# Group weight sums of a down-projection: GpSimd subtractions against DMAs that add from DRAM

## The chip, the cores and the metric

One Trainium2 chip, and of it one core. The metric is the device time of one execution of the whole kernel in microseconds (us). A profile of one execution is taken beside the timed runs. The engines are TensorE (PE; its weight loads PEld), VectorE (DVE), ScalarE (ACT), GpSimd (POOL) and SyncE (SP), each with an instruction queue of its own that is worked in order; SP, ACT and POOL also issue DMAs.

## The reference

One layer of a decoder trunk on 1024 tokens of width 1024, in float32: a norm, two attentions whose outputs are gated and merged, a residual add, then a norm and a gated MLP with a short causal convolution, a residual add, and a last norm. The change lies in the last product of the MLP:

```python
def conv_ffn(xn, w_up, conv_w, conv_b, w_down):
    S = xn.shape[1]
    u = xn @ w_up
    upad = jnp.pad(u, ((0, 0), (CONV_WIDTH - 1, 0), (0, 0)))
    c = conv_b
    for j in range(CONV_WIDTH):
        c = c + upad[:, j:j + S] * conv_w[j]
    gate, val = jnp.split(c, 2, axis=-1)
    return (jax.nn.silu(gate) * val) @ w_down      # 1024x2816 times 2816x1024
...
        x = x + conv_ffn(xn, w_up[l], conv_w[l], conv_b[l], w_down[l])
    return rmsnorm(x, norm_final_w)
```

## The kernel before, in words

All data lie transposed: channels on the 128 partitions, tokens along the free dimension. Each float32 product is made of three matmuls on rounded parts: high weight by high operand, high weight by low operand, low weight by high operand. A weight tile of 128x1024 (`raw`) gets its high part `wh` by a cast on ScalarE (L161) and its low part `wl` by a subtraction on VectorE (L163); `wh` and `wl` have two buffers each, so a weight can be split once the group two before it is done on TensorE. Operands are split into `h` in the same way, by halves of 128x512 (L835 on ScalarE, L836 on VectorE).

The down-projection (`down`) has 22 chunks of hidden channels. Six are multiplied plainly (`pieces`, L1117). The other sixteen form a 2x2 block product by a Strassen-like scheme with seven products, the stages P1, P5, P6, P3, P7, P2, P4 in this order. Each stage has four groups m (128 output channels each), and each group 8 x 3 matmuls of 128x512 (`product`, L1166). The weight of a stage is a quarter of the weight matrix or a sum of quarters, the operand a quarter of the hidden values or a sum of quarters. With A11, A12 the upper quarters (left, right) and A21, A22 the lower ones as the code's `quarter(m, right, below)` addresses them, where `right` picks the later hidden chunks and `below` the later output channels:

- P5 takes S1 = quarter(left, below) + quarter(right, below). `group_first` makes it in tile `S` (one of four buffers, one for each m): a load from SP (L112), then a DMA from GpSimd's queue that adds from DRAM (L113).
- P6 takes S2 = S1 - quarter(left, above), P3 takes S4 = quarter(right, above) - S2, P7 takes S3 = quarter(left, above) - quarter(left, below). `group_raw` loads the quarters into `raw` buffers (three of them) through SP (L151), and `group_sum` subtracts on GpSimd (L99 for P6, L101 for P3, L104 for P7), in place in `S` for P6 and P3 and in place in a `raw` buffer for P7.
- P1, P2 and P4 take plain quarters, loaded into `raw`.

`next_w` hands out the next weight and `ahead` prepares two groups in advance, with the raw loads of one more. `prep` makes the operands, two a group: `operand` sums hidden quarters in place on VectorE (L1031 for P5, L1033 for P6, L1038 for P7, L1042 for P4) and `parts_h` splits the result into one of 20 `h` buffers. The hidden quarters come from DRAM through SP (`fetch_h`, L1009) into `ha`, `hb`, `hc`, eight buffers each. After a group its sum is added to the output tile `x3` (`evict`, L1173), and where an output is complete, `norm` squares it on ScalarE (L1155), adds the squares on VectorE (L1157) and scales by the norm weight on ScalarE (L1158). The running sum of squares, `acc`, takes an `S` buffer once the first of them is free; the squares take tiles `c` of 128x1024, of which there are two (before, the convolution used them).

The order of the instructions on each engine is fixed when the kernel is built, by a planner: it simulates the kernel with costs of its own and takes, of what is ready on an engine, that which stands first in the program. So operands of a later stage can run in an earlier one (the P4 operands of L1042 ran in P5), and loads are issued as soon as their buffers are free. The waits on the chip follow from the real times; an instruction whose input is late holds all that is queued behind it on its engine.

Of the kernel before, what the change touches and what calls it, by code (L numbers as in the profile page):

```python
# [13 lines left out]
ALU = mybir.AluOpType  # L14
# [3 lines left out]
P = 128  # L18
# [4 lines left out]
H2 = 512  # L23
# [20 lines left out]
class Trunk:  # L44
# [24 lines left out]
    def ahead(self, n):  # L69
        while len(self.wq) < n and self.wsrc and (self.wsrc[0][1] != "pair" or self.uw):  # L70
            src, nk, *eng = self.wsrc.pop(0)
            if nk == "grp":
                self.wq.append(self.load_w(None, 8, raw=self.group_sum(*src, eng[0] if eng else self.group_raw(*src))))
            elif nk == "pair":
                first, skip = eng or (False, 0)
                self.wq.append(self.split_pair(*self.sum_pair(src, first), skip))
            else:
                self.wq.append(self.load_w(src, nk, *eng))
        if self.deep and self.wsrc and len(self.wsrc[0]) == 2 and not isinstance(self.wsrc[0][1], str):

            src, nk = self.wsrc[0]
            self.wsrc[0] = src, nk, None, None, self.load_raw(src, nk)
        elif self.deep and self.wsrc and self.wsrc[0][1] == "grp" and len(self.wsrc[0]) == 2:
            src, nk = self.wsrc[0]
            self.wsrc[0] = src, nk, self.group_raw(*src)

    def quarter(self, m, right, below):
        return self.w_dn[m + 4 * below, :, N1 + 8 * right:N1 + 8 * right + 8, :]

    def group_raw(self, name, m):  # L90

        parts = {"P5": (), "P6": ((0, 0),), "P3": ((1, 0),), "P7": ((0, 0), (0, 1))}[name]
        return [self.load_raw(self.quarter(m, *p), 8) for p in parts]

    def group_sum(self, name, m, raws):

        s, tt = self.S[m], self.nc.gpsimd.tensor_tensor
        if name == "P6":
            tt(s, s, raws[0], ALU.subtract)  # L99
        elif name == "P3":  # L100
            tt(s, raws[0], s, ALU.subtract)  # L101
        elif name == "P7":
            s = raws[0]
            tt(s, s, raws[1], ALU.subtract)  # L104
        return s

    def group_first(self, m):

        nc = self.nc
        s = self.tl(self.uw, [P, KC, P], "S", bufs=4)  # L110
        flat = lambda t: t.rearrange("p k c -> p (k c)")
        nc.sync.dma_start(flat(s), flat(self.quarter(m, False, True)))  # L112
        nc.gpsimd.dma_start(flat(s), flat(self.quarter(m, True, True)), accum_op=ALU.add)  # L113
        self.S.append(s)

    def sum_pair(self, src, first=False, idle=None):


        nc = self.nc
        g = self.tl(self.wp, [P, 2, 4, P], "raw", bufs=RAW)  # L120
        nc.sync.dma_start(g.rearrange("p a k c -> p (a k) c"), src[0])
        v = self.tl(self.wp, [P, 2, 4, P], "raw", bufs=RAW) if first and not idle else self.tl(self.uw, [P, 2, 4, P], idle or "rv", bufs=2)
        nc.sync.dma_start(v.rearrange("p a k c -> p (a k) c"), src[1])
        sa, sb = (self.tl(self.sfp[0], [P, 2, 4, P], self.sfp[1]) for _ in range(2))
        tt = nc.gpsimd.tensor_tensor
        tt(sa[:, 0], v[:, 0], v[:, 1], ALU.add)  # L126
        tt(sa[:, 1], sa[:, 0], g[:, 0], ALU.subtract)  # L127
        tt(sb[:, 0], g[:, 0], v[:, 0], ALU.subtract)  # L128
        tt(sb[:, 1], g[:, 1], sa[:, 1], ALU.subtract)
        return g, v, sa, sb  # L130
# [895 lines left out]
    def operand(self, stage, k):  # L1026

        tt, R = self.nc.vector.tensor_tensor, self.R
        a = R["B11", k]
        if stage == "P5":  # L1030
            tt(a, R["B12", k], a, ALU.subtract)  # L1031
        elif stage == "P6":
            tt(a, R["B22", k], a, ALU.subtract)  # L1033
        elif stage == "P3":
            a = R["B22", k]
        elif stage == "P7":
            a = R["B12", k]
            tt(a, R["B22", k], a, ALU.subtract)  # L1038
        elif stage == "P2":
            a = R["B21", k]  # L1040
        elif stage == "P4":
            tt(a, R["B21", k], a, ALU.subtract)  # L1042
        self.B[stage, k] = self.parts_h(a)

    def glu(self, j, w, us, tp, after):
# [29 lines left out]
    def down(self):  # L1075

        nc, tc = self.nc, self.tc
        with ExitStack() as ctx:
# [6 lines left out]
            tt = nc.vector.tensor_tensor  # L1085
# [60 lines left out]
            acc = []  # L1146

            def norm(m, hf, a=0, b=H2):

                if not acc:  # L1150
                    acc.append(self.tl(self.uw, [P, 2, H2], "S", bufs=4))
                x = x3[:, m, hf * H2 + a:hf * H2 + b]
                sum_ = acc[0][:, hf, a:b]
                sq = sum_ if m == 0 else self.tl(self.cpl, [P, b - a], "c")
                nc.scalar.activation(sq, x, AF.Square)  # L1155
                if m and (m < KC - 1 or hf):
                    tt(sum_, sum_, sq, ALU.add)  # L1157
                nc.scalar.mul(x, x, self.vecs[:, C_NO + m:C_NO + m + 1])  # L1158
                return sq
# [10 lines left out]
            def evict(ps, to, done):  # L1170
                for m, hf in to:
                    x = col(m, hf)
                    tt(x, x, ps, ALU.add)  # L1173
                    if done:
                        norm(m, hf)
# [36 lines left out]
            for a, b in ((0, q), (q, H2)):  # L1212
                for m, w in zip((2, 3), ws):
                    ps = chains[1][m][:, a:b]
                    product(ps, w, "P4", False, a, b, lambda k, m=m: tail.pop(0)() if a and k == (4 if m < 3 else 2) else None)
                    for f in owed:
                        f()
                    owed = []
                    x = x3[:, m + 4, a:b]
                    tt(x, x, ps, ALU.add)  # L1220
                    sq = norm(m + 4, 0, a, b)
                    while not a and tail:
                        tail.pop(0)()
                tail = self.last_norm(psD, [acc[0][:, 0, a:b], sq], x3, 0, a, b, ((0, 1, nc.vector), (1, 3, nc.vector), (6, 8, nc.gpsimd), (3, 6, nc.vector)) if a else
                                      ((0, 3, nc.gpsimd), (3, 5, nc.vector), (5, 8, nc.vector)))
# [98 lines left out]
```

## Time and profile before

| | us |
|---|---|
| median of 3 runs | 1338.62 |
| lowest and highest | 1336.24, 1339.04 |
| the profiled execution | 1338.15 |
| its span in the profile | 1336.4 |
| first matmul of P1, of P5, of P6, of P3, of P7 (us from the span's start) | 1164.0, 1185.7, 1208.5, 1230.2, 1257.0 |

How to read the rows that follow: in the waits, "engine line waited for" is followed by total us, times and the longest in us. In a table of stretches each engine has its busy us and number of instructions; then come the granted clock of TensorE as a share of full speed, the mean busy share of the 16 DMA engines, and GB/s. In a timeline a row has start, duration, engine, line, operation, tiles (out<-in) and number; in brackets the idle time before it and what ended it. In a group row, the busy us and the mean ns of one stand behind the bar, then the idle time before. DMA issues are listed with their number, size and the median us from issue to landing.

### The profile page before, as it was taken

The numbers are of one execution on the slowest core, as the hardware profiler recorded it, in microseconds if no ns is written. First come the engines' busy times: TensorE is split into PE (matmuls) and PEld (weight loads), VectorE is DVE, ScalarE is ACT, GpSimd is POOL, SyncE is SP. The second block draws the span as 40 slices with busy tenths as digits, with TensorE's granted clock in tenths as the row PEclk, the third lists the DMA queues.
The fourth block names the chain that finished last, engine by engine and source line by source line (L and its number), as shares of the span: only waits on it lengthen the run. The fifth ranks groups of instructions, "written<-read, shape, count | busy, mean of one in ns | idle before, by whom it ended". The sixth has DMA issues, their size and how long they took to land.

```text
span 1336.4 us, 17027 instructions
## 1 busy us (share of the span) xinstructions
PE 1317.7 (99%) x6256; PEld 1097.9 (82%) x6256; DVE 1064.3 (80%) x1429; ACT 606.2 (45%) x937; POOL 503.1 (38%) x364
## 2 busy tenths in 40 slices
PE   8999999999999999999999999999999999999997
PEld 6888888888888878888888888888888888888786
DVE  7847776289888976445669999999999997889664
ACT  8432232276667774333444343434343434334443
POOL 0346652000101015641446666666656620135111
PEclk9999999999999999999999999999999999999998
DMA  7244443976554246324423122222222229934242
GB/s 259 107 146 159 148 151 126 266 179 186 146 137 141 83 137 225 120 106 142 146 92 110 64 94 80 80 78 89 86 79 79 75 96 354 270 116 129 64 148 104
DMA packets 63091, 180.26 MB, mean 135 GB/s; under 512 B 6944, under 2 KB 16800, under 8 KB 63008
## 3 DMA queue, kind: packets, MB, share of 16 engines
q1 hardware_dynamic: 50976, 159.90, 36.4%
q10 hardware_dynamic: 11456, 17.18, 3.5%
q0 software_dynamic: 576, 2.10, 0.8%
q8 instruction: 49, 0.80, 0.2%
q14 instruction: 34, 0.28, 0.1%
HBM read 130.39 MB, written 48.76 MB: 134 GB/s over the span
## 4 chain that ended last, share of the span: by engine, by line
PE 95%; DVE 2%; ACT 1%; issue 1%; DMA 0%; POOLq 0%; POOL 0%; ACTq 0%
PE t L916 44%; PE y L1166 6%; PE g L182 4%; PE g L183 4%; PE g L184 4%; PE d L1166 4%; PE sc L184 3%; PE sc L183 3%; PE sc L182 3%; PE sc L648 3%; PE y L1117 2%; PE d L1117 2%; PE t L664 1%; DVE h L836 1%; PE t L767 1%; PE t L309 1%
## 5 line engine op out<-in xcount | busy, mean ns | idle before, releaser
L1060 POOL TENSOR_TENSOR us<-us,rstd 128x1024 f32<-128x1024 f32 x42 | 92.3, 2216 | 82.4 <-DVE us L481 47.6
L1069 ACT ACTIVATE c<-us,vecs 128x1024 f32<-128x1024 f32 x44 | 54.8, 1247 | 127.2 <-POOL us L1060 121.6
L161 ACT CAST wh<-raw 128x1024 fp32r<-128x1024 f32 (+1 forms) x53 | 53.9, 1016 | 102.3 <-PE sc L183 35.5
L142 DVE TENSOR_TENSOR sl<-sf,sh 128x1024 fp32r<-128x1024 f32 x62 | 89.3, 1441 | 12.8 <-ACT sh L140 12.8
L163 DVE TENSOR_TENSOR wl<-raw,wh 128x1024 fp32r<-128x1024 f32 (+1 forms) x53 | 70.4, 1331 | 36.3 <-ACT wh L161 26.6
L140 ACT CAST sh<-sf 128x1024 fp32r<-128x1024 f32 x62 | 64.5, 1042 | 61.6 <-PE t L916 44.0
L126 POOL TENSOR_TENSOR sf<-rv 128x512 f32<-128x512 f32 x30 | 50.4, 1681 | 93.5 <-DVE sl L142 59.0
L1166 PE MATMUL y<-h,wh 128*128 128x512 f32 (+1 forms) x288 | 80.8, 366 | 0.0
L1071 DVE SCALAR_TENSOR_TENSOR c<-us,vecs,c 128x1024 f32<-128x1024 f32 x44 | 74.4, 1724 | 5.8 <-ACT c L1069 5.7
L128 POOL TENSOR_TENSOR sf<-raw,rv 128x512 f32<-128x512 f32 x30 | 56.8, 1892 | 46.3 <-DVE sl L142 46.3
L1072 DVE SCALAR_TENSOR_TENSOR c<-us,vecs,c 128x1024 f32<-128x1024 f32 x44 | 73.2, 1697 | 0.0
L182 PE MATMUL g<-xh,wh 128*128 128x512 f32 x176 | 71.0, 403 | 1.5 <-ACT g L577 1.5
L183 PE MATMUL g<-xl,wh 128*128 128x512 f32 x176 | 70.3, 400 | 0.0
L184 PE MATMUL g<-xh,wl 128*128 128x512 f32 x176 | 70.2, 399 | 0.0
L1052 ACT ACTIVATE c<-c 128x1024 f32<-128x1024 f32 x22 | 23.4, 1063 | 88.5 <-DVE c L1072 88.5
L631 POOL MEMSET aT<- 128x128 f32 x32 | 6.1, 204 | 151.6 <-PE t L677 63.1
L652 DVE CUSTOM_DVE_ANT_0 L<-sc,bias 128x128 f32<-128x128 f32 (+7 forms) x64 | 47.8, 752 | 16.6 <-PE sc L648 13.7
L1166 PE MATMUL d<-h,wh 128*128 128x512 f32 x192 | 60.6, 397 | 0.0
L142 DVE TENSOR_TENSOR wl<-raw,wh 128x1024 fp32r<-128x1024 f32 (+1 forms) x32 | 59.7, 1864 | 0.1
L1166 PEld LDWEIGHTS y<-h,wh 128*128 128x128 f32 x288 | 52.1, 189 | 8.8
L127 POOL TENSOR_TENSOR sf<-sf,raw 128x512 f32<-128x512 f32 x31 | 58.2, 1876 | 2.2
L653 ACT ACTIVATE L<-L,sm 128x128 f32<-128x128 f32 (+7 forms) x64 | 49.6, 778 | 20.0 <-DVE sm L652 17.3
(413 smaller groups left out, 4282.0 us busy)
## 6 DMA issues: line engine op xcount, KB each, us to landing
u<-qd SPq DMA_DIRECT2D x72, 256.0 KB, 6.6
raw<-in_w_down SPq DMA_DIRECT2D x28, 512.0 KB, 3.5
raw<-in_w_up SPq DMA_DIRECT2D x23, 512.0 KB, 3.5
raw<-in_w_in SPq DMA_DIRECT2D x22, 512.0 KB, 4.1
hd<-c SPq DMA_DIRECT2D x22, 512.0 KB, 2.6
rv<-in_w_up SPq DMA_DIRECT2D x21, 512.0 KB, 3.5
gr<-gd SPq DMA_DIRECT2D x16, 512.0 KB, 3.4
qd<-us SPq DMA_DIRECT2D x15, 512.0 KB, 2.6
```

The lines of the kernel that those rows point to most:

```text
L127: tt(sa[:, 1], sa[:, 0], g[:, 0], ALU.subtract)
L140: cast = nc.scalar.copy(hi, src)
L142: low = nc.vector.tensor_tensor(lo, src, hi.bitcast(F32), ALU.subtract)
L163: self.lo = (eng or nc.vector).tensor_tensor(wl, raw, wh.bitcast(F32), ALU.subtract)
L182: nc.tensor.matmul(ps, wh[:, kc + o, :], ah, start=first and n == 0, stop=False)
L183: nc.tensor.matmul(ps, wh[:, kc + o, :], al, start=False, stop=False)
L184: nc.tensor.matmul(ps, wl[:, kc + o, :], ah, start=False, stop=last and n == len(kcs) - 1)
L916: nc.tensor.matmul(ps, (ah, ah, al)[p][:, k, :], (bh, bl, bh)[p], start=first and n == p == 0, stop=last and p == 2 and n == len(ks) - 1, ...
L1060: i = (nc.vector if m % NF == 0 else nc.gpsimd).tensor_tensor(us[:, 2:], us[:, 2:], self.rstd, ALU.mult)
L1071: nc.vector.scalar_tensor_tensor(c, us[:, 1:T + 1], cw[1], c, ALU.mult, ALU.add)
L1072: nc.vector.scalar_tensor_tensor(c, us[:, 0:T], cw[0], c, ALU.mult, ALU.add)
L1166: nc.tensor.matmul(ps, v[:, k, :], x, start=start and k == i == 0, stop=k == 7 and i == 2, skip_group_check=True)
```

## The change

The sums are made in place in `S` by DMAs that add from DRAM, issued on GpSimd's queue right after the split of the group's weight is traced. After P5, `S` (S1) changes sign on ScalarE and quarter(left, above) is added: it holds -S2. After P6, quarter(right, above) is added: S4. After P3, SP loads quarter(left, below) into `S`, ScalarE changes its sign and quarter(left, above) is added: S3. As P6 now takes -S2, its operand changes sign too, and P4's operand, which is made from it, adds where it subtracted. No sum is made on GpSimd itself any more, and the groups use no `raw` buffers and no loads ahead. Since `S` is now in use until P7, the running sum of squares and the squares move to two tiles `c`: `acc[0]`, and `acc[1]` whose two halves take turns.

```diff
             if nk == "grp":
-                self.wq.append(self.load_w(None, 8, raw=self.group_sum(*src, eng[0] if eng else self.group_raw(*src))))
+                name, m = src
+                self.wq.append(self.load_w(None, 8, raw=self.S[m]))
+                self.group_next(name, m)
...
-        elif self.deep and self.wsrc and self.wsrc[0][1] == "grp" and len(self.wsrc[0]) == 2:
-            src, nk = self.wsrc[0]
-            self.wsrc[0] = src, nk, self.group_raw(*src)
...
-    def group_raw(self, name, m):
-
-        parts = {"P5": (), "P6": ((0, 0),), "P3": ((1, 0),), "P7": ((0, 0), (0, 1))}[name]
-        return [self.load_raw(self.quarter(m, *p), 8) for p in parts]
-
-    def group_sum(self, name, m, raws):
-
-        s, tt = self.S[m], self.nc.gpsimd.tensor_tensor
-        if name == "P6":
-            tt(s, s, raws[0], ALU.subtract)
-        elif name == "P3":
-            tt(s, raws[0], s, ALU.subtract)
-        elif name == "P7":
-            s = raws[0]
-            tt(s, s, raws[1], ALU.subtract)
-        return s
+    def add_to(self, s, src):
+        flat = lambda t: t.rearrange("p k c -> p (k c)")
+        self.nc.gpsimd.dma_start(flat(s), flat(src), accum_op=ALU.add)
...
     def group_first(self, m):
 
-        nc = self.nc
         s = self.tl(self.uw, [P, KC, P], "S", bufs=4)
-        flat = lambda t: t.rearrange("p k c -> p (k c)")
-        nc.sync.dma_start(flat(s), flat(self.quarter(m, False, True)))
-        nc.gpsimd.dma_start(flat(s), flat(self.quarter(m, True, True)), accum_op=ALU.add)
+        self.nc.sync.dma_start(s, self.quarter(m, False, True))
+        self.add_to(s, self.quarter(m, True, True))
         self.S.append(s)
 
+    def group_next(self, name, m):
+
+        nc, s = self.nc, self.S[m]
+        if name == "P7":
+            return
+        if name == "P3":
+            nc.sync.dma_start(s, self.quarter(m, False, True))
+        if name != "P6":
+            nc.scalar.mul(s, s, -1.0)
+        self.add_to(s, self.quarter(m, name == "P6", False))
...
         elif stage == "P6":
-            tt(a, R["B22", k], a, ALU.subtract)
+            tt(a, a, R["B22", k], ALU.subtract)
...
         elif stage == "P4":
-            tt(a, R["B21", k], a, ALU.subtract)
+            tt(a, R["B21", k], a, ALU.add)
...
                 if not acc:
-                    acc.append(self.tl(self.uw, [P, 2, H2], "S", bufs=4))
+                    acc.extend(self.tl(self.cpl, [P, 2, H2], "c") for _ in range(2))
                 x = x3[:, m, hf * H2 + a:hf * H2 + b]
                 sum_ = acc[0][:, hf, a:b]
-                sq = sum_ if m == 0 else self.tl(self.cpl, [P, b - a], "c")
+                sq = sum_ if m == 0 else acc[1][:, m % 2, a:b]
```

## The prediction

> **What bounds the kernel now.** First the page's head, then what TensorE waited for, over the whole span.
>
> ```profile
> span 1336.4 us, 17027 instructions
> PE 1317.7 (99%) x6256; PEld 1097.9 (82%) x6256; DVE 1064.3 (80%) x1429; ACT 606.2 (45%) x937; POOL 503.1 (38%) x364
> ...
> PE t L309 <- ACT wh L339: 4.7, 1, 4.7
> PE d L1166 <- DVE wl L163: 3.5, 2, 3.0
> ```
>
> TensorE is busy all but 18.7 us. GpSimd work is worth nothing by itself; the change can pay only where GpSimd makes TensorE wait. The second wait is such a place: the grouped down-projection (L1166) waits twice for VectorE's low part of a weight (wl). Next, busy time by stretches, cut where the matmuls turn from one stage to the next: P5, P6, P3, P7.
>
> ```profile
> core 0: us, PE busy (x) PEld busy (x) DVE busy (x) ACT busy (x) POOL busy (x), PEclk, DMA share, GB/s
> 1185.70:1208.40 22.70, 22.18 (x98) 18.02 (x97) 20.48 (x21) 8.94 (x14) 11.57 (x4) 1.00 0.49 151
> 1208.40:1230.20 21.80, 21.80 (x97) 17.76 (x96) 19.77 (x20) 8.64 (x13) 11.88 (x4) 1.00 0.38 115
> 1230.20:1257.10 26.90, 23.89 (x99) 19.33 (x98) 19.18 (x23) 12.04 (x19) 3.85 (x2) 0.94 0.23 73
> 1257.10:1278.90 21.80, 21.80 (x98) 18.06 (x97) 15.92 (x20) 12.03 (x19) 4.80 (x2) 1.00 0.46 145
> ```
>
> The stages hold 96 matmuls each. P6 and P7 take 21.8 us without a gap; P5 takes 0.9 more, P3 5.1 more. That 6.0 us is all there is to win here. P3's 5.1 is 3.0 idle (26.90 - 23.89) and 2.1 of slower matmuls (23.89 - 21.80), as TensorE's timeline and clock show:
>
> ```profile
> 1235.78 0.61 PE L1166 MATMUL d<-h,wh 128*128 128x512 f32 x2
> 1239.41 0.50 PE L1166 MATMUL d<-h,wl 128*128 128x512 f32 x1 [3.01 <-DVE wl L163]
> ...
> 1240.87 1.06 PE L1166 MATMUL d<-h,wh 128*128 128x512 f32 x2
> ...
> 1243.39 0.62 PE L1166 MATMUL d<-h,wh 128*128 128x512 f32 x2
> ...
> 1240.00:1244.00 4.00, 4.00 (x12) 0.58 0.13 51
> ```
>
> Why was wl late? VectorE's timeline up to it, with two undisturbed rows, then GpSimd's:
>
> ```profile
> 1181.33 1.23 DVE L163 TENSOR_TENSOR wl<-S,wh 128x1024 fp32r<-128x1024 f32 x1 [0.17 <-ACT wh L161]
> ...
> 1226.00 3.40 DVE L163 TENSOR_TENSOR wl<-S,wh 128x1024 fp32r<-128x1024 f32 x1 [0.21 <-ACT wh L161]
> 1229.33 4.70 DVE L836 TENSOR_TENSOR h<-hb,h 128x512 fp32r<-128x512 f32 x4
> ...
> 1235.76 2.46 DVE L836 TENSOR_TENSOR h<-hc,h 128x512 fp32r<-128x512 f32 x1
> 1238.14 1.21 DVE L163 TENSOR_TENSOR wl<-S,wh 128x1024 fp32r<-128x1024 f32 x1
> ...
> 1254.35 2.49 DVE L836 TENSOR_TENSOR h<-hc,h 128x512 fp32r<-128x512 f32 x4
> ```
>
> ```profile
> 1190.80 3.98 POOL L99 TENSOR_TENSOR S<-S,raw 128x1024 f32<-128x1024 f32 x1 [5.38 <-DVE wl L163]
> ...
> 1225.91 2.42 POOL L104 TENSOR_TENSOR raw<-raw,raw 128x1024 f32<-128x1024 f32 x1 [3.71 <-DMA raw<-in_w_down]
> 1228.27 3.40 POOL L101 TENSOR_TENSOR S<-raw,S 128x1024 f32<-128x1024 f32 x1
> ...
> 1235.30 2.38 POOL L104 TENSOR_TENSOR raw<-raw,raw 128x1024 f32<-128x1024 f32 x1 [3.62 <-DMA raw<-in_w_down]
> ```
>
> Whenever a GpSimd sum runs, one VectorE instruction beside it loses about 2 us: 3.40 for 1.23 (2.2), 4.70 for four at 2.49 (2.2), 2.46 for 0.62, a quarter of that (1.8). Together 6.2 us. Without them the late wl would start at 1238.14 - 6.2 = 1231.9 and end at 1233.2; TensorE wanted it at 1239.41 - 3.01 = 1236.4.
>
> **The change, part by part.** *GpSimd sums out.* Twelve go:
>
> ```profile
> L101 POOL TENSOR_TENSOR S<-raw,S 128x1024 f32<-128x1024 f32 x4 | 13.8, 3446 | 8.1 <-DVE wl L163 8.1
> L99 POOL TENSOR_TENSOR S<-S,raw 128x1024 f32<-128x1024 f32 x4 | 11.6, 2890 | 30.1 <-DVE wl L163 30.1
> L104 POOL TENSOR_TENSOR raw<-raw,raw 128x1024 f32<-128x1024 f32 x4 | 9.6, 2399 | 33.4 <-DMA raw<-in_w_down 33.4
> ```
>
> The 35.0 us of GpSimd was never waited for directly, so its own worth is 0; its worth is the VectorE time. P3's stall goes whole (margin 1236.4 - 1233.2 = 3.2 us), and with it the slow matmuls: 5.1 us. P5's stall hangs on this piece of the chain that ended last:
>
> ```profile
> 1188.98 0.61 DVE h L836
> 1189.61 3.04 DMA hc<-hd
> 1192.67 1.58 DVE ha L1042
> ```
>
> That split frees the buffer which the load fills. VectorE was about 2 us late there by the same kind of collision, and the sum at 1190.80 disturbs the operand behind it again. With two times 2 us back against a gap of 0.52, the 0.9 us go too. Next on VectorE is nothing: its 20.5, 19.8 and 19.2 us in the three stages, less some 2 us for each of ten sums, leave about a third of it idle.
>
> *ScalarE sign turns in.* Eight (four after P5, four after P3), priced by these rows of the page:
>
> ```profile
> L1069 ACT ACTIVATE c<-us,vecs 128x1024 f32<-128x1024 f32 x44 | 54.8, 1247 | 127.2 <-POOL us L1060 121.6
> L161 ACT CAST wh<-raw 128x1024 fp32r<-128x1024 f32 (+1 forms) x53 | 53.9, 1016 | 102.3 <-PE sc L183 35.5
> ```
>
> So 1.0 to 1.25 us each; I take 1.25, the row with a scale in it. Four make 5.0 us in a stage where ScalarE is busy 9 to 12 us of 21.8. Behind a sign turn stand the next cast (wh) and the h casts. A weight buffer comes free one group (21.8 / 4 = 5.44 us) before its use, the wl is used only two matmuls (2 x 21.8 / 96 = 0.45 us) into its group, and cast (1.0) and wl (1.23) take, with their handovers, about 2.4 us; that leaves 5.44 + 0.45 - 2.4 = 3.5 us, which covers one sign turn. Cost 0; without that cover up to 8 x 1.25 = 10 us. After P5 the turn waits for VectorE's wl, which is due earlier than now.
>
> *Loads.* SP loses 16 loads of raw and gains four of S after P3, each waiting for that group's wl. On SP behind them stand loads of the P2 and P4 weights, which have three free raw buffers and tens of us: cost 0. GpSimd's queue gains 12 adding DMAs.
>
> ```profile
> raw<-in_w_down SPq DMA_DIRECT2D x28, 512.0 KB, 3.5
> ...
> S<-in_w_down SPq DMA_DIRECT2D x4, 512.0 KB, 6.0
> S<-in_w_down POOLq DMA_DIRECT2D x4, 512.0 KB, 9.7
> ...
> L113 POOL DMA_DIRECT2D S<-in_w_down x4: 862/882/1061, 1152.7 to 1161.1; - x4
> ...
> DMA to landing us min/median/max: 8.2/9.7/11.9
> ```
>
> Issuing takes 0.9 us, 10.6 in all, with nothing behind on that queue but further adds and the norm's rstd, stages later. No adding DMA runs in a quiet stretch, so its landing is bounded by a plain load (3.5) and the slowest add (11.9, in the busiest stretch); I take 9.7, its own row. Chain to the next stage: after P5, 1.25 + 0.9 + 9.7 = 11.9 us; after P6 less; after P3, with a reload of 3.5 to 6.0, 15.4 to 17.9. From a group's wl to the cast of the same group one stage on there are 21.8 - 2.4 = 19.4 us, 22.9 before TensorE waits. Covered: cost 0.
>
> *Signs, norm tiles.* The P6 and P4 operands stay one VectorE instruction each. The norm's squares alternate between two halves of one tile where two buffers alternated, 5.4 us apart in use: cost 0, or 0.6 us (an add of 128x512, half a wl) where one had to wait.
>
> **Sum.** 1338.15 (profiled execution; span 1336.4) - 5.1 - 0.9 = 1332.15. That execution lies 0.5 below the median of 1338.62, so 1332.6 against the median. The one reading in doubt is the 2.1 us. The Trainium skill, "TensorE: Matmul & The Clock Gate", section "HAM oscillation — how this bites in real kernels", warns of idle gaps above about 3.4 us. Here 3.01 us of idleness stand before a granted clock of 0.58, so trace and figure differ; by the figure the slow stretch would have another cause and the sum would be 1334.7.
>
> **The rivals.** *A: the clock dip is not the stall's.* Then only 3.9 us go: 1334.7. Against it: the first matmuls after the gap are the slow ones. The page named above is what speaks for it.
>
> *B: ScalarE held by the reload.* The planner decides when the kernel is built whether the sign turn of a P3 group stands ahead of the next group's wh cast. If ahead, ScalarE sits through the reload and the groups form a loop: landing, turn 1.25, cast 1.05, wl 1.23, some 0.2 of handover. At 3.5 us landing it takes 7.2 against 5.44: 4 x 1.76 - 3.5 slack = 3.5 us given back, 1336.1, just inside no change. For it: the reload comes due (2.4 + 3.5 = 5.9 us after the buffer is free) close to the next cast (5.44). Against it: a planner that knows the 3.5 puts the cast first.
>
> *C: the same loop at the 6.0 us of S loads.* 9.7 against 5.44: 17 - 3.5 = 13.5 us, 1346.1, slower. It decides from a landing of 4.8 us, where the loss passes 6.0 + 2.7. Against it: 6.0 is from the busiest stretch; P3's DMA share is 0.23.
>
> *D: the adding chain after P3 is late.* At the slowest rows 7.1 + 1.25 + 1.06 + 11.9 = 21.3 of 22.9 us (7.1 is the slowest landing of the S loads); twice the middle landings, 2 x (6.0 + 9.7) + 2.1 = 33.5, would start P7 10.6 us late, with another clock dip of 2.1 at 1332.6 + 12.7 = 1345. The 7.1 is here:
>
> ```profile
> L112 SPq DMA_DIRECT2D S<-in_w_down x4: 382/383/430, 1147.4 to 1148.9; - x4
> ...
> DMA to landing us min/median/max: 4.6/6.0/7.1
> ```
>
> Four issues took at most 1.06 us beside a busy VectorE. The Trainium skill, "SBUF — State Buffer", section "A bandwidth-pool intuition that's wrong (but worth ruling out)", has a GpSimd-issued DMA go from 620 to 3100 ns beside some VectorE copies; by that, as an estimate, the 21.3 would be 23.8 and D would hold. The issue rows speak against it here.
>
> *E: nothing moves.* VectorE's order is planned anew and another late instruction takes the place of the sums: about 1338.
>
> **How the numbers follow.** A measurement of this kernel tells about 0.2% (2.7 us) from no change. Forecast 0.52, A 0.06: faster 0.58. B 0.15, E 0.07: same 0.22. C 0.14, D 0.06: slower 0.20. Forecast alone: 1330 to 1335 (all of the 6.0 and the runs' own 2.8 us spread below, A's price above). The range runs 1329.8 to 1341; what is left out is most of C and D and a little below.
>
> **What would show it.** In the changed profile: no L1166 wait of TensorE on wl; P5, P6 and P3 at 21.8 us with clock 1.00; wl from S near 1.23 us throughout and four h splits at 2.49; eight new ScalarE instructions of about 1.25; 16 adding DMAs. Wrong would be: ScalarE idle on the S load ahead of a wh cast (B, C), a wh cast waiting for an adding DMA (D), VectorE still slow with GpSimd idle, or a wl late behind a new order (E).

## The result, and the profile after

The changed kernel takes 1332.00 us in the median (1331.47 to 1332.21, 6 runs) against 1338.47 (6 runs of the kernel before beside it): a ratio of 0.9955, 95% interval 0.9943 to 0.9968. The profiled execution took 1331.87 us, its span 1330.1.

What TensorE waited for over the whole span of the changed kernel, longest first (total us, times, longest):

```profile
PE t L304 <- ACT wh L334: 5.1, 1, 5.1
PE g L177 <- ACT g L572: 1.5, 4, 0.5
PE d L200 <- POOL rs L194: 1.1, 1, 1.1
```

The wait of the grouped products on wl is gone from the list; the first entry is a wait at the start of the kernel that stood there before with 4.7 us. The stretches of P5, P6, P3 and P7 in the changed kernel (busy us and number of PE, PEld, DVE, ACT, POOL, then clock, DMA share, GB/s):

```profile
1185.70:1207.50 21.80, 21.80 (x98) 18.06 (x97) 15.07 (x22) 12.31 (x17) 3.46 (x4) 1.00 0.77 157
1207.50:1229.30 21.80, 21.80 (x98) 18.06 (x97) 14.76 (x21) 8.93 (x13) 2.61 (x3) 1.00 0.73 157
1229.30:1251.10 21.80, 21.80 (x98) 18.06 (x97) 11.22 (x15) 13.69 (x19) 3.47 (x4) 1.00 0.72 147
1251.10:1272.90 21.80, 21.80 (x97) 18.02 (x97) 16.40 (x23) 14.18 (x23) 0.00 (x0) 1.00 0.20 47
```

All four are full, and the clock is 1.00 in P3, where it was 0.94. VectorE's busy time in P5 and P3 fell from 20.5 and 19.2 us to 15.1 and 11.2 (P3 is also shorter now, and holds 15 VectorE instructions where the longer stretch held 23). The 6.0 us sit where they were looked for: in the chain that ended last, the first block of P2 starts here in the kernel before and in the one after.

```profile
1278.91 10.88 PE d L1166 x48
```

```profile
1273.07 10.88 PE d L1161 x48
```

That is 5.84 us of the 6.3 by which the spans differ. P1 starts 0.16 us later in the changed kernel (1164.27 for 1164.11 in the same two chains), so from P1 to P2 the gain is 6.0. The other 0.46 lies at the very end of the execution, in a piece that the chain calls issue (1.16 us for 1.62) and that the change doesn't touch. VectorE at the start of P3 in the changed kernel, the place of the long stall:

```profile
1225.00 1.23 DVE L158 TENSOR_TENSOR wl<-S,wh 128x1024 fp32r<-128x1024 f32 x1 [0.17 <-ACT wh L156]
1226.15 2.49 DVE L831 TENSOR_TENSOR h<-hb,h 128x512 fp32r<-128x512 f32 x4
...
1230.96 1.22 DVE L158 TENSOR_TENSOR wl<-S,wh 128x1024 fp32r<-128x1024 f32 x1
```

The same instructions in the same order as before, but 1.23 for 3.40 and 2.49 for 4.70; the second wl ends at 1232.2, and the matmul that uses it starts 3.1 us later, at 1235.3. And what was put in: adding DMAs (L91), reloads (L106) and sign turns (L108) of tile S.

```profile
L91 POOL DMA_DIRECT2D S<-in_w_down x16: 856/866/1082, 1155.1 to 1249.3; - x16
...
L158 DVE TENSOR_TENSOR wl<-S,wh x16: 1218/1225/1226, 1181.5 to 1263.1; 128x1024 fp32r<-128x1024 f32 x16
L108 ACT ACTIVATE S<-S x8: 1054/1061/1064, 1183.2 to 1247.8; 128x1024 f32<-128x1024 f32 x8
```

```profile
S<-in_w_down POOLq DMA_DIRECT2D x12, 512.0 KB, 5.6
hc<-hd SPq DMA_DIRECT2D x8, 256.0 KB, 5.6
S<-in_w_down SPq DMA_DIRECT2D x4, 512.0 KB, 4.3
```

A sign turn takes 1.06 us, an add is issued in 0.87 and lands after 5.6, a reload after 4.3. Every wl from S takes 1.23 us at most. Issuing the adds doesn't slow VectorE: four splits took their 2.49 us from 1204.39 on while GpSimd issued an add from 1204.87 to 1205.74. On ScalarE in P3 of the changed kernel the planner put the sign turn behind the next cast:

```profile
1234.80 1.05 ACT L156 CAST wh<-S 128x1024 fp32r<-128x1024 f32 x1 [2.85 <-PE d L1161]
1236.39 1.06 ACT L108 ACTIVATE S<-S 128x1024 f32<-128x1024 f32 x1 [0.54 <-DMA S<-in_w_down]
```

The turns wait for their reloads, this one by 0.54 us and the longest by 1.10, but each with the cast already done.

### The profile page after: what moved, and what is told of

It reads as the page before. It is cut to its first block, busy times and chain, and to the rows that moved or that the text cites. A ratio compares the mean times of both kernels' runs of the same rounds, so it can differ in the third digit from the quotient of the medians.

```text
span 1330.1 us, 17018 instructions
## 1 busy us (share of the span) xinstructions
PE 1314.5 (99%) x6256; PEld 1096.5 (82%) x6256; DVE 1049.4 (79%) x1429; ACT 614.1 (46%) x945; POOL 477.2 (36%) x364
## 4 chain that ended last, share of the span: by engine, by line
PE 98%; ACT 1%; DVE 1%; issue 0%; DMA 0%; POOLq 0%; POOL 0%; SPq 0%; ACTq 0%
PE t L911 44%; PE y L1161 7%; PE d L1161 5%; PE g L177 4%; PE g L178 4%; PE g L179 4%; PE sc L179 3%; PE sc L177 3%; PE sc L178 3%; PE sc L643 3%; PE y L1112 2%; PE d L1112 2%; PE t L659 1%; PE t L762 1%; PE t L304 1%; PE sc L731 1%
## 5 line engine op out<-in xcount | busy, mean ns | idle before, releaser
L158 DVE TENSOR_TENSOR wl<-raw,wh 128x1024 fp32r<-128x1024 f32 (+1 forms) x49 | 66.0, 1350 | 35.1 <-ACT wh L156 25.4
L156 ACT CAST wh<-raw 128x1024 fp32r<-128x1024 f32 (+1 forms) x49 | 49.7, 1014 | 93.4 <-PE sc L178 35.4
L121 POOL TENSOR_TENSOR sf<-rv 128x512 f32<-128x512 f32 x30 | 46.6, 1554 | 94.9 <-DVE sl L137 60.1
L137 DVE TENSOR_TENSOR wl<-raw,wh 128x1024 fp32r<-128x1024 f32 (+1 forms) x32 | 59.7, 1864 | 2.0 <-ACT wh L135 2.0
```

Of the source, the lines that this page charges most:

```text
L137: low = nc.vector.tensor_tensor(lo, src, hi.bitcast(F32), ALU.subtract)
L158: self.lo = (eng or nc.vector).tensor_tensor(wl, raw, wh.bitcast(F32), ALU.subtract)
```

## The experiments

One theory and two rivals went in. T: GpSimd's sums slow VectorE beside them, wl comes late, TensorE stalls, and its clock dips behind the long stall. The rivals: L, the gain comes from the loads taken off SP's queue; C, the clock dip has another cause than the stall.

**All sums out of the kernel before.**

```diff
         if name == "P6":
-            tt(s, s, raws[0], ALU.subtract)
+            pass
         elif name == "P3":
-            tt(s, raws[0], s, ALU.subtract)
+            pass
         elif name == "P7":
             s = raws[0]
-            tt(s, s, raws[1], ALU.subtract)
```

> The kernel before with the twelve GpSimd sums left out (the group weights are then wrong, all loads and splits stay). Theory T (the sums slow VectorE beside them, so wl is late in P5 and P3, TensorE stalls, and its clock dips after the long stall): the whole 6.0 us goes, about 1332.4; P5, P6, P3 at 21.8 us each. Rival L (the gain of the change comes from the 16 loads and raw buffers taken off SP's queue): nothing moves, 1338.5. Rival C (the clock dip is not the stall's): 3.9 us go, 1334.6, and a dip stays in P3.

Measured: 1333.73 us (ratio to the kernel before 0.9971, 0.9962 to 0.9981). P6, P3 and P7 are full at clock 1.00; this is P3:

```profile
1231.00:1252.80 21.80, 21.80 (x98) 18.06 (x97) 12.93 (x18) 11.74 (x19) 0.00 (x0) 1.00 0.08 24
```

In P5 a stall of 1.4 us is left, larger than the 0.5 before. Its rows, from TensorE's waits and from the chain that ended last:

```profile
PE d L1165 <- DVE wl L162: 1.4, 1, 1.4
```

```profile
1188.68 6.12 DMA hc<-hd
```

With no sum to read them, the raw buffers come free at once and their loads go out in a burst (ten are issued from 1172.5 to 1188.6 us, where the kernel before issues three up to 1185.8), and the hidden quarter that VectorE waits for in P5 takes 6.12 us in place of 3.04. T holds for P3; the P5 stall has a second parent, that load. C falls: the dip went with the stall.

**Only the P7 sums out, and only the P6 sums out.** The two edits are the last and the first of the three above.

> The kernel before with only the four sums of P7 left out (L104; S3 is then wrong). T: two of the three sums beside P3's late wl are these; VectorE gets back 2.2 + 1.8 = 4.0 us of its 6.2, more than the 3.0 us of the stall, so P3 falls to 21.8 us and P5 keeps its 0.9: 1338.5 - 5.1 = 1333.4. L: 1338.5. C: 1335.5.

> The kernel before with only the four sums of P6 left out (L99; S2 and what is made from it are then wrong). T: these run in P5; P5's 0.9 us goes and P3 keeps its 5.1: 1337.6. L: 1338.5. If a sum costs the same wherever it runs (a third of 6.0): 1336.5.

Measured: 1333.34 (ratio 0.9967, 0.9956 to 0.9977) without the P7 sums, 1337.18 (0.9994, 0.9985 to 1.0004, so not clear of no change) without the P6 sums. TensorE's wait on wl in the one and in the other:

```profile
PE d L1165 <- DVE wl L162: 0.5, 1, 0.5
```

```profile
PE d L1166 <- DVE wl L163: 3.4, 1, 3.4
```

The one leaves P5's half us, with P3 full at a clock of 1.00; the other leaves P3's stall and nothing in P5. Four sums are worth 5 us or about 1, by where they run (the 1 by the profile, as the times alone don't settle it). L is out: each of these kernels keeps all sixteen loads.

**The sums on VectorE.**

```diff
-        s, tt = self.S[m], self.nc.gpsimd.tensor_tensor
+        s, tt = self.S[m], self.nc.vector.tensor_tensor
```

> The kernel before with the twelve sums on VectorE in place of GpSimd, loads and all else as before. T: a sum takes VectorE 1.2 us and costs it about 2 us where GpSimd makes it, so VectorE is ahead by some 10 us over the stages; no wait on wl beyond a few tenths: 1332.4 to 1333.4. L: 1338.5. If VectorE's own load is what makes wl late: above 1338.5.

Measured: 1332.16 (1331.81 to 1332.30; ratio 0.9959, 0.9944 to 0.9974), no wait on wl at all. One of the twelve, in VectorE's timeline of this run:

```profile
1233.06 1.22 DVE L104 TENSOR_TENSOR raw<-raw,raw 128x1024 f32<-128x1024 f32 x1
```

VectorE does in 1.22 us what GpSimd did in 2.4 to 5.2 while holding VectorE up. A change of one word gives what the adding DMAs give: the gain is in taking the sums off GpSimd, not in where they go.

**Three GpSimd sums in a row put into the changed kernel.**

```diff
+                if name == "P3" and m == 0:
+                    for _ in range(3):
+                        d = self.load_raw(self.quarter(m, False, False), 8)
+                        self.nc.gpsimd.tensor_tensor(d, d, w[0].bitcast(F32), ALU.subtract)
```

> The changed kernel with three such GpSimd sums in a row at the start of P3 (results unused). T: VectorE loses about 6.2 us between the wl of the first and of the second group, against 3.3 us of margin: a stall of 2.9 us in front of the second group's first wl matmul and a clock dip of about 2 us behind it: 1332.0 + 5.0 = 1337.0. Rival L: no change, 1332.0. Rival C: a stall without a dip, 1334.9.

Measured: 1337.09 (ratio to the kernel before 0.9989, 0.9979 to 0.9999), 5.1 above the changed kernel. VectorE, GpSimd and TensorE at the place:

```profile
1225.90 9.12 DVE L836 TENSOR_TENSOR h<-hb,h 128x512 fp32r<-128x512 f32 x4
```

```profile
1224.81 9.06 POOL L80 TENSOR_TENSOR raw<-raw,wh 128x1024 f32<-128x1024 f32 x3 [2.98 <-ACT wh L161]
```

```profile
1238.62 0.79 PE L1166 MATMUL d<-h,wl 128*128 128x512 f32 x1 [3.42 <-DVE wl L163]
```

Four splits that take 2.49 us undisturbed took 9.12 beside three sums, 2.2 us more for each sum, and the stall is back. So is the dip, in TensorE's busy time, matmuls and clock behind the stall:

```profile
1238.60:1242.60 4.00, 3.98 (x9) 0.50 0.91 227
1242.60:1246.60 4.00, 4.00 (x15) 0.78 0.58 142
```

The edit adds three loads too, but none of them stands in the chain that ended last. That is T from the other side.

**Twelve GpSimd sums, one a group, put into the changed kernel.**

```diff
+                if name != "P7":
+                    d = self.load_raw(self.quarter(m, False, False), 8)
+                    self.nc.gpsimd.tensor_tensor(d, d, w[1].bitcast(F32), ALU.subtract)
```

> The changed kernel with twelve GpSimd sums of 128x1024 put back beside it, one a group after the wl of P5, P6 and P3, each on a freshly loaded raw buffer and its result unused. T: each takes about 2 us of VectorE, but never more than one a group, under the 3.2 to 3.5 us of slack, so no wait on wl: 1332 to 1333. If a sum costs by its number: 6.0 more, 1338.

Measured: 1340.72 (ratio to the kernel before 1.0017, 1.0008 to 1.0027). A miss: spread out they cost 8.7 us, more than the clump. ScalarE from the end of P3 into P7 shows part of how:

```profile
1243.08 1.06 ACT L112 ACTIVATE S<-S 128x1024 f32<-128x1024 f32 x1 [4.97 <-DMA S<-in_w_down]
...
1256.11 1.06 ACT L112 ACTIVATE S<-S 128x1024 f32<-128x1024 f32 x1 [6.58 <-DMA S<-in_w_down]
...
1260.80 1.04 ACT L160 CAST wh<-S 128x1024 fp32r<-128x1024 f32 x1
```

A late wl makes the reload late, the sign turn waits for it on ScalarE, and behind the turn stands the cast of a P7 group, for which TensorE then waits:

```profile
1261.90 0.77 PE L1165 MATMUL y<-h,wh 128*128 128x512 f32 x2 [2.16 <-ACT wh L160]
```

With 0.98 us more on that group's wl and a dip of the clock behind it, this place costs the most; gaps of 0.5, 1.1 and 0.2 us in P5, P6 and P3 come before it. Two more runs took sums and loads apart: one with a single loaded buffer for all twelve sums, one with the twelve loads and no sum.

```diff
+                if name == "P5" and m == 0:
+                    self.spare = self.load_raw(self.quarter(m, False, False), 8)
+                if name != "P7":
+                    d = self.spare
+                    self.nc.gpsimd.tensor_tensor(d, d, w[1].bitcast(F32), ALU.subtract)
```

> The run before with twelve spaced sums and twelve loads came out at 1340.7, not at 1332 to 1333: its stalls lay in P6 and P7, where a wh cast stood behind a sign turn that waited for a reload of 5.5 to 7.1 us. This one keeps the twelve GpSimd sums and takes their loads away (one loaded buffer serves all; results unused). If the landings made slow by the extra loads are the cause: 1332 to 1334. If the sums' slowing of VectorE alone is the cause (wl late, so reload, turn and cast late): 1338 to 1341. If it takes both: between, about 1335.

```diff
+                if name != "P7":
+                    self.load_raw(self.quarter(m, False, False), 8)
```

> The changed kernel with the twelve extra loads alone, nothing reading them. Landings as the cause: 1338 or more, with sign turns waiting for the reload ahead of wh casts. Sums as the cause: 1332. As the kernel before carries sixteen such loads, theory T expects 1332 to 1334.

Measured: 1337.07 with the sums (ratio 0.9993, 0.9983 to 1.0003), 1340.25 with the loads (1.0016, 1.0006 to 1.0026). Sums alone, the third to fifth wl in VectorE's timeline from the end of P6 on:

```profile
1238.50 2.82 DVE L164 TENSOR_TENSOR wl<-S,wh 128x1024 fp32r<-128x1024 f32 x1
...
1245.45 2.52 DVE L164 TENSOR_TENSOR wl<-S,wh 128x1024 fp32r<-128x1024 f32 x1 [2.01 <-ACT wh L162]
...
1249.11 2.81 DVE L164 TENSOR_TENSOR wl<-S,wh 128x1024 fp32r<-128x1024 f32 x1
```

Loads alone, the chain that ended last and TensorE's timeline in P5:

```profile
1189.28 10.43 DMA hc<-hd
```

```profile
1202.21 0.79 PE L1163 MATMUL d<-h,wl 128*128 128x512 f32 x1 [4.55 <-DVE wl L160]
```

Either is enough, in different places. The loads, with nothing to hold them back, go out in a burst (ten from 1172 to 1188 us); the hidden quarter for P5 lands after 10.43 us, VectorE waits for it with wl queued behind, and TensorE stops for 4.55, with a dip of the clock of 6.8 us that starts near the end of the stop. The sums hurt through small gaps in P5, P6 and P7, with the chain from wl to reload to turn to cast passing the delay on, and with no dip of the clock. The waits list gives them 2.8 us, but it counts only from the end that the profile puts to a matmul; counted between the starts of the matmuls on either side they cost 0.8, 1.1 and 2.0, together 3.9, and P2 starts 4.3 us later than in the changed kernel. What is left of the 5.1 us isn't settled. The two together (8.7) are less than the sum of both (5.1 + 8.2): in the combined run the sums free the raw buffers one by one and so pace the loads (from 1172 to 1186 us three are issued, not ten, and the hidden quarter takes 4.92 us).

**Gaps of four lengths in the changed kernel.** For the third group of P5, P6, P3 and P7, n = 4, 5, 6, 7 unused sums on VectorE are queued ahead of wl.

```diff
+                    for _ in range(n):
+                        i = vt(d, d, wh.bitcast(F32), ALU.subtract)
...
+                    with self.tc.issue_after(i.ins):
+                        self.lo = vt(wl, s, wh.bitcast(F32), ALU.subtract)
```

> The changed kernel with 4, 5, 6 and 7 unused VectorE sums of 1.14 us ahead of the wl of the third group of P5, P6, P3 and P7. With 3.5 us of slack TensorE should stop for about 1.1, 2.2, 3.3 and 4.5 us. T with the one dip seen: a clock dip of about 2 us behind the gaps of 3 us and more, none behind the shorter. By the 3.4 us of the Trainium skill (TensorE: Matmul & The Clock Gate): behind the last alone. C: behind none. Time with two dips: 1332 + 11 + 4 = 1347.

Measured: 1358.36 in one run. TensorE's timeline at the four gaps (each has another 0.46 us some matmuls ahead, waiting for the cast):

```profile
1200.19 0.68 PE L1174 MATMUL d<-h,wl 128*128 128x512 f32 x1 [1.57 <-DVE wl L86]
...
1227.72 0.80 PE L1174 MATMUL y<-h,wl 128*128 128x512 f32 x1 [3.12 <-DVE wl L86]
...
1255.57 0.79 PE L1174 MATMUL d<-h,wl 128*128 128x512 f32 x1 [3.48 <-DVE wl L86]
```

```profile
1286.50 0.79 PE L1174 MATMUL y<-h,wl 128*128 128x512 f32 x1 [5.21 <-DVE wl L86]
```

The clock behind the first three (busy TensorE, matmuls, clock):

```profile
1200.00:1204.00 4.00, 3.81 (x10) 0.57 0.66 148
1204.00:1208.00 4.00, 4.00 (x19) 1.00 0.98 179
...
1227.70:1231.70 4.00, 3.98 (x11) 0.58 0.82 178
1231.70:1235.70 4.00, 4.00 (x19) 1.00 1.03 197
...
1255.50:1259.50 4.00, 3.93 (x9) 0.50 0.92 273
1259.50:1263.50 4.00, 4.00 (x14) 0.71 0.44 126
```

A dip stands behind all four, also behind 0.46 + 1.57 = 2.0 us. In stretches of 1 us the clock is 0.50 inside each; the 0.57 and 0.58 are means over 4 us. By these means the halved clock lasts 4.0 x 0.43 x 2 = 3.4 us behind each of the first two gaps, and in finer stretches 6.8 behind each of the other two. Idle time (13.4 + 4 x 0.46 = 15.2) and half of the dips (10.2) make up 25.4 of the 26 us above the changed kernel. The gaps came out longer than aimed at: four extra sums in a row took 5.0 us, not 4 x 1.14 = 4.6, and from the second gap on evictions and adds of the norm ran between them. C is out, and so is the notion that about 3 us is the least that dips.

**The sign turn ahead of the cast.** This run tests the prediction's rivals B and C.

```diff
+                hold = self.turn if (name, m) in (("P3", 1), ("P3", 2), ("P3", 3), ("P7", 0)) else None
+                with self.tc.issue_after(hold.ins) if hold else nullcontext():
+                    w = self.load_w(None, 8, raw=self.S[m])
```

> The changed kernel with each wh cast of the second to fourth group of P3, and of the first of P7, held behind the sign turn of the group before. This is rivals B and C of the prediction made real. With the changed kernel's own rows, landing 4.3, turn 1.06, cast 1.05, wl 1.23 and 0.2 of handover, the loop is 7.85 us against 5.44: 4 x 2.4 - 3.5 = 6.1 us, 1338. If ScalarE's place in the order is of no account: 1332.

Measured: 1339.44 (ratio to the kernel before 1.0011, 1.0001 to 1.0020), 7.4 above the changed kernel. ScalarE in P3:

```profile
1239.52 1.06 ACT L111 ACTIVATE S<-S 128x1024 f32<-128x1024 f32 x1 [2.82 <-DMA S<-in_w_down]
1240.49 1.03 ACT L159 CAST wh<-S 128x1024 fp32r<-128x1024 f32 x1
...
1248.37 1.06 ACT L111 ACTIVATE S<-S 128x1024 f32<-128x1024 f32 x1 [3.58 <-DMA S<-in_w_down]
1249.33 1.03 ACT L159 CAST wh<-S 128x1024 fp32r<-128x1024 f32 x1
```

The casts follow each other at 1249.33 - 1240.49 = 8.84 us, where a group takes 5.44: the reloads took up to 5.5 us here, not 4.3. TensorE's longest stop for such a cast:

```profile
1250.41 0.73 PE L1164 MATMUL d<-h,wh 128*128 128x512 f32 x2 [2.30 <-ACT wh L159]
```

So the place of one ScalarE instruction in the order would have undone the whole gain.

## Why the prediction was right

The forecast was 1332.6 us, the time 1332.0, inside the forecast's own 1330 to 1335.

- **What bounds the kernel.** Right: the stalls of P5 and P3, 6.0 us, went whole, and nothing else of size moved. Of the two stalls the long one is shown from both sides (the P7 sums out, three sums put back). The dip of the clock, the 2.1 us in doubt, went with the stall and came back with it, so rival A falls.
- **GpSimd sums out.** The mechanism was right, and the margin of 3.2 us in P3 came out as 3.1. Too large was the amount elsewhere: VectorE's busy time fell by 14.9 us (1064.3 to 1049.4), not by the twenty that 2 us for each of ten sums make; a sum beside an idle VectorE takes nothing from it.
- **P5's 0.9 us.** Right as a term, thinner as a reason, and so in part luck. It was put down to VectorE being late beside the sums; a late load of the hidden quarter brings the same stall, as the 1.4 us without any sum show. In the changed kernel these loads land later than before (5.6 us against 3.3 in the stretch from P5 to P7), beside adds and with a DMA share of 0.77 in P5 for 0.49, and the wl for P5's third group is ready 1.2 us before its use. With the extra loads alone it was not.
- **Sign turns.** 1.06 us against 1.25 taken. Covered, as said: no wait of TensorE in these stages is left.
- **Loads and adds.** The add landed after 5.6 us, not 9.7; the reload after 4.3, in the range of 3.5 to 6.0. The chain after P3, 4.3 + 1.06 + 0.87 + 5.6 = 11.8 us, has room in the 22.9. Rival D did not come near, and the four issues that spoke for 0.9 us were borne out by sixteen at 0.86 to 1.08; the 3100 ns that the Trainium skill, "SBUF — State Buffer", section "A bandwidth-pool intuition that's wrong (but worth ruling out)", gives beside some VectorE copies did not show in these issues. The stretch from P5 to P7 put it to no real test: what VectorE ran there were additions and subtractions of two tiles, no copies.
- **Rivals B and C.** The planner put the cast first. Their price was right in kind: the forced order cost 7.4 us, between the 3.5 and the 13.5 worked out for landings of 3.5 and 6.0, at up to 5.5. In size it was somewhat too high: four casts on, from 1224.24 to 1257.95, the loop took 33.7 us where four groups take 21.8, and 11.9 less the 3.5 of slack would be 8.4.
- **Rival E.** The order of VectorE's instructions at the start of P3 stayed as it was.

## What to carry to other kernels

Where one engine's work slows another's, count not the busy time but the margin of the instruction that somebody waits for: the same sum cost 0 or several us by whether its victim stood ahead of a wl with 3 us in hand. Before an elaborate way round, try the plain one; the twelve sums on VectorE itself did as well as adding DMAs. Slack taken group by group doesn't add up when a late step passes its delay on (wl, reload, turn, cast), and a removed reader can set loads free that then crowd out the one that matters.

## What the runs showed of the hardware that was not expected

TensorE's clock was halved behind idle times of 2.0, 3.0, 3.1, 3.5 and 5.2 us, and not behind 0.5 (P5 of the kernel before), 1.36 (P5 with all sums out) or 0.82 + 0.53 (the forced order). The Trainium skill, "TensorE: Matmul & The Clock Gate", section "HAM oscillation — how this bites in real kernels", sets the mark at about 3.4 us; the gaps of 2.0 to 3.1 us here disagree with that number. Behind the gap of 2.0 us, 10 matmuls ran in 3.81 us where 17 of 0.227 fit: a stall of 2 us cost about 1.6 us more. The ten dips in these stages, over all runs, lasted 3.4 us (five of them) or 6.8 us (the other five), nothing between; half of that is what a dip costs. What decides between the two isn't shown: 3.4 us stood behind gaps of 2.0 to 3.4 us, 6.8 behind gaps of 3.1 (2.16 + 0.98) to 5.2.

A GpSimd sum of 128x1024 that runs beside a VectorE subtraction of two tiles costs VectorE about 2.2 us (3.40 for 1.23 beside one, 9.12 for 2.49 beside three), nearly the 2.4 us of the shortest sum; and GpSimd loses too, as the same sum took up to 5.19 us. The issue of an adding DMA from the same engine, 0.87 us, leaves VectorE at its full speed.
